# A gated product on one core: loads and stores dealt out by tile to two DMA queues instead of one queue for each direction

## The chip, the core and the metric

The kernel runs on one core of a Trainium2 chip. A core has a tensor engine (PE), a vector engine (VectorE, DVE in the profile), a scalar engine (ScalarE, ACT), a general engine (GpSimd, POOL) and a sync engine (SyncE, SP), each with its own stream of instructions. Data move between the chip's main memory (HBM) and the core's memory of 128 partitions (SBUF) by DMA: an instruction on SP or ACT issues a transfer, which then runs on 16 DMA engines that all of the core's queues share. The profile calls the queue of SP's transfers q1 and that of ACT's q10. Waits go by semaphores, which an instruction or a landed transfer raises.

The metric is the device time of one execution in microseconds (us), less is better. Times are the median of several executions; the profile comes from one further execution of the same program.

## The reference

The input is 8192 x 8192 in 32-bit floats. The left half of the columns is multiplied by the sigmoid of the right half:

```python
def reference(x):
    a, b = np.split(x, 2, axis=-1)
    return a * (1 / (1 + np.exp(-b)))
```

So 268.4 MB are read and 134.2 MB are written, and each element takes one sigmoid and one product.

## The kernel before

The 8192 rows are cut into 32 tiles of 256 rows. Each of the 128 partitions holds two whole rows of a tile, which lie next to each other in HBM: 64 KB a partition, 8 MB a tile. The result of a tile is half as large, 32 KB a partition and 4 MB. There are two input buffers (`x_sb0`, `x_sb1`) and two output buffers (`o_sb0`, `o_sb1`); even tiles use the first of each, odd tiles the second.

For each tile the work is a load, a sigmoid in place over the right halves on ACT (L92), the product in two pieces (L97), and a store. The product of the first 3/16 of the columns is done by POOL (by DVE in tile 1), and that of the rest by DVE, which starts when POOL is done. The first and the last tile are worked on in fourths (half a row each, all products on DVE) so that a store can start earlier. Tile 0 is loaded in two transfers, one for each of the two rows of a partition, and stored in two; tile 31 is stored in three pieces (one half, two quarters), of which each is issued one fourth late.

A helper, `place`, drops all dependences but those that are listed, and keeps the program's order on each engine. Four waits are left:

- load i+2 waits for the last product of tile i, which frees the input buffer (`free`, L62);
- the sigmoid of tile i waits for the landing of load i and, from tile 2 on, of store i-2, which frees the output buffer. Both are joined by an empty instruction on PE (`met`, L87), so that ACT waits for one semaphore;
- the product follows the sigmoid, DVE's piece follows POOL's;
- store i waits for the products of tile i (`done`, L69).

All loads are issued by SP (L63), all stores by ACT (L68), so loads stand in one queue and stores in the other. The order of the instructions is written out by the last loop of `_tiles`: the work of tile i, then load i+2, then what is left to store of tile i. ACT's stream thus has, tile after tile, the sigmoid and then the store, at which ACT stands until the product is done. Loads 0 and 1 are issued ahead of the loop, without waits. After the program is built, `_launch_early` moves the first load on SP to before the start barrier, and `_close_on_sync` writes the end anew: the last store's semaphore is awaited on SP, all the others on POOL.

Of the kernel before, what the change touches and what calls it, by code (L numbers as in the profile page):

```python
# [8 lines left out]
def _tiles(ctx, tc, x, out):  # L9
    nc = tc.nc  # L10
    P = nc.NUM_PARTITIONS
    DEP = mybir.DependencyInfo(mybir.DependencyClass.Sync, mybir.DependencyReason.DATA)
    fp32 = mybir.dt.float32
    SIG = mybir.ActivationFunctionType.Sigmoid

    n_rows, n_cols = x.shape
    half = n_cols // 2
    R = 2
    SLOTS = 2
    n_tiles = n_rows // (P * R)  # L20
    x_g = x.rearrange("(g p h r) m -> g h p (r m)", p=P, h=2, r=R)
    out_g = out.rearrange("(g p h r) m -> g h p (r m)", p=P, h=2, r=R)

    pool = ctx.enter_context(tc.tile_pool(name="io", bufs=1))
    xs = [pool.tile([P, R * n_cols], fp32, name=f"x_sb{k}") for k in range(SLOTS)]
    os = [pool.tile([P, R * half], fp32, name=f"o_sb{k}") for k in range(SLOTS)]

    whole = [(0, 8)]
    rows = [(0, 4), (4, 8)]
    cut = half // 16 * 3  # L30
    few_and_most = [(0, 8, 0, cut), (0, 8, cut, half)]
    fourths = [(k, k + 2, k % 4 * half // 4, (k % 4 + 2) * half // 4) for k in range(0, 8, 2)]
    loads = [whole] * n_tiles
    works = [few_and_most] * n_tiles
    stores = [whole] * n_tiles
    behind = [0] * n_tiles
    loads[0] = stores[0] = rows
    works[0] = works[-1] = fourths
    stores[-1] = [(0, 4), (4, 6), (6, 8)]
    behind[-1] = 1  # L40

    def meet(a, b):
        return a[0] < b[1] and b[0] < a[1]

    traced = [[] for _ in range(SLOTS)]
    load_of, mul_of, store_of = {}, {}, {}

    def place(i, ins, *needs):


        kept = {n.ins.name for n in needs}
        for e in traced[i % SLOTS]:
            if e.ins.name not in kept:
                tc.declare_no_dep(ins.ins, e.ins, reason="follows from the waits that are kept")
        traced[i % SLOTS].append(ins)
        tc.keep_in_program_order(ins)
        return ins

    def load(i):
        for lo, hi in loads[i]:  # L60
            c = slice(lo * n_cols // 4, hi * n_cols // 4)
            free = [m for w, m in mul_of.get(i - SLOTS, []) if meet(w, (lo, hi))]  # L62
            ins = nc.sync.dma_start(out=xs[i % SLOTS][:, c], in_=x_g[i // 2, i % 2, :, c])  # L63
            load_of.setdefault(i, []).append(((lo, hi), place(i, ins, *free)))

    def store(i, lo, hi):
        c = slice(lo * half // 4, hi * half // 4)
        ins = nc.scalar.dma_start(out=out_g[i // 2, i % 2, :, c], in_=os[i % SLOTS][:, c])  # L68
        done = [m for w, m in mul_of[i] if meet(w, (lo, hi))]  # L69
        store_of.setdefault(i, []).append(((lo, hi), place(i, ins, *done)))  # L70

    def work(i, lo, hi, near, far):

        rows = xs[i % SLOTS].rearrange("p (r h m) -> p r h m", r=R, h=2)
        packed = os[i % SLOTS].rearrange("p (r m) -> p r m", r=R)
        r, c = slice(lo // 4, (hi + 3) // 4), slice(near, far)
        b = rows[:, r, 1, c]
        landed = [s for w, s in load_of[i] if meet(w, (lo, hi))]
        gone = [s for w, s in store_of.get(i - SLOTS, []) if meet(w, (lo, hi))]
        middle = 0 < i < n_tiles - 1  # L80
        rest = middle and near
        if rest:
            before = mul_of[i].pop()[1]
        else:
            g = rows[:, r, 1, :] if middle else b
            if middle and gone:
                met = nc.tensor.nop(nofuse=True)  # L87
                for n in (*landed, *gone):
                    tc.add_manual_dep(met.ins, n.ins.name, DEP, reason="joins the waits")
                place(i, met, *landed, *gone)  # L90
                landed = [met]
            before = nc.scalar.activation(out=g, in_=g, func=SIG)  # L92
            for n in landed:
                tc.add_manual_dep(before.ins, n.ins.name, DEP, reason="both have landed")
            place(i, before, *landed)
        engine = nc.gpsimd if far == cut and i > 1 else nc.vector
        mul = engine.tensor_mul(out=packed[:, r, c], in0=rows[:, r, 0, c], in1=b)  # L97
        tc.add_manual_dep(mul.ins, before.ins.name, DEP, reason="follows the gate, or the first columns")
        place(i, mul, before, *(() if middle else gone))
        mul_of.setdefault(i, []).append(((lo, hi), mul))  # L100

    for i in range(SLOTS):
        load(i)
    for i in range(n_tiles):
        due = list(stores[i])
        for k, piece in enumerate(works[i]):
            work(i, *piece)
            ready = works[i][k - behind[i]][1] if k >= behind[i] else 0
            while len(stores[i]) > 1 and k < len(works[i]) - 1 and due[0][1] <= ready:
                store(i, *due.pop(0))  # L110
        if i + SLOTS < n_tiles:
            load(i + SLOTS)
        for lo, hi in due:
            store(i, lo, hi)


def _launch_early(nc):
# [68 lines left out]
@with_exitstack  # L186
def kernel(
    ctx: ExitStack,
    tc: tile.TileContext,
    x: bass.AP,  # L190
    out: bass.AP,
):
    nc = tc.nc
    with ExitStack() as pools:
        _tiles(pools, tc, x, out)
    tc.close()
    tc.compile()
    _launch_early(nc)
    _close_on_sync(nc)
# [30 lines left out]
```

## Time and profile before

| | us |
|---|---|
| median of 3 executions | 932.75 (932.47 to 932.77) |
| the profiled execution, its time | 932.44 |
| its span, from the first instruction to the last | 931.1 |
| DVE busy | 232.5 |
| ACT busy | 227.0 |
| POOL busy | 99.3 |
| the sigmoid of a whole tile on ACT | 7.03 |
| POOL's piece of a product | 3.42 |
| DVE's piece of a product | 7.09 |
| a load, from issue to landing, median | 40.0 |
| a store of 4 MB, from issue to landing, median | 40.2 |

The page of the profile gives busy times for each engine, the share of DMA time in 40 slices of the span as digits (9 is 90% or more), the packets of each DMA queue, the chain of work that ended last, and the transfers by line with the time from issue to landing. A transfer's issue is short (0.3 to 0.4 us); its data move afterwards on the 16 engines, and its packets are recorded there with a start and a duration. The time from issue to landing includes what lies ahead of the transfer in its queue. Lines such as L92 are line numbers of the kernel before. "ACTq" and "SPq" are the streams of ACT and SP where they issue transfers.

### The profile page before, as it was taken

The page shows a single profiled execution, that of the slowest core. Times are in us where ns is not written, and L with a number is a line of the kernel's source. Part 1 is how long each engine was busy: PE and PEld are TensorE (multiplying, and loading weights), DVE is VectorE, ACT ScalarE, POOL GpSimd, SP SyncE. Part 2 cuts the span into 40 slices and gives each one's busy share as a digit, 9 for nine tenths or more (in the row PEclk, how much of TensorE's full clock was granted, in tenths as well). Part 3 has the DMA queues.
Part 4 walks back from the last instruction along what each step waited for, and adds up shares of the span by engine and source line. Part 5 has one row for each costly group of instructions (what it writes and reads, how often), then busy time and mean ns, then how long its engine had stood idle before and what let it go on. Part 6 is the DMA issues. An engine that isn't in the chain of part 4 may idle for free.

```text
span 931.1 us, 299 instructions
## 1 busy us (share of the span) xinstructions
DVE 232.5 (25%) x39; ACT 227.0 (24%) x39; POOL 99.3 (11%) x33
## 2 busy tenths in 40 slices
DVE  1133203332023320233302333023330233311333
ACT  2123332033320333202332023320233202333023
POOL 0001110111101111011110111101111011110110
DMA  9999999999999999999999999999999999999998
GB/s 405 450 442 414 428 450 425 453 405 428 450 428 450 410 469 405 428 450 428 450 405 459 420 428 451 425 450 408 431 448 428 450 408 467 408 428 450 427 452 383
DMA packets 9793, 402.67 MB, mean 432 GB/s; under 512 B 1088, under 2 KB 1088, under 8 KB 1088
## 3 DMA queue, kind: packets, MB, share of 16 engines
q1 hardware_dynamic: 4752, 268.44, 66.6%
q10 hardware_dynamic: 5040, 134.22, 33.4%
q14 instruction: 1, 0.01, 0.0%
HBM read 268.44 MB, written 134.22 MB: 432 GB/s over the span
## 4 chain that ended last, share of the span: by engine, by line
DMA 69%; DVE 12%; ACT 12%; POOL 5%; issue 0%; PEldq 0%; ACTq 0%; SPq 0%
DMA out_dram<-o_sb 60%; DVE o_sb L97 12%; ACT x_sb L92 12%; DMA x_sb<-in_x_dram 9%; POOL o_sb L97 5%; PEldq L87 0%; ACTq L68 0%; SPq L63 0%
## 5 line engine op out<-in xcount | busy, mean ns | idle before, releaser
L97 DVE TENSOR_TENSOR o_sb<-x_sb 128x6656 f32<-128x6656 f32 (+2 forms) x39 | 232.5, 5969 | 690.3 <-POOL o_sb L97 632.7
L92 ACT ACTIVATE x_sb<-x_sb 128x8192 f32<-128x8192 f32 (+1 forms) x38 | 225.7, 5949 | 692.7 <-PEq L87 632.9
L97 POOL TENSOR_TENSOR o_sb<-x_sb 128x1536 f32<-128x1536 f32 x29 | 99.1, 3417 | 793.9 <-ACT x_sb L92 793.9
L92 ACT ACT_TABLE_LOAD x1 | 1.3, 1283 | 0.8 <-PEq L214 0.8
L214 POOL MEMSET const-float32-0.0<- 128x1 f32 x1 | 0.1, 99 | 0.2 <-issue 0.2
L214 POOL MEMSET const-bfloat16-1.0<- 128x1 bf16 x1 | 0.1, 103 | 0.0
L214 POOL MEMSET const-uint8-127<- 128x1 uint8 x1 | 0.1, 103 | 0.0
L214 POOL MEMSET const-float32-1.0<- 128x1 f32 x1 | 0.1, 99 | 0.0
## 6 DMA issues: line engine op xcount, KB each, us to landing
out_dram<-o_sb ACTq DMA_DIRECT2D x30, 4096.0 KB, 40.2
x_sb<-in_x_dram SPq DMA_DIRECT2D x2, 4096.0 KB, 16.6
out_dram<-o_sb ACTq DMA_DIRECT2D x3, 2048.0 KB, 27.8
out_dram<-o_sb ACTq DMA_DIRECT2D x2, 1024.0 KB, 8.3
x_sb<-in_x_dram SPq DMA_DIRECT2D x31, 40.0
```

What stands on the lines that cost most here:

```text
L92: before = nc.scalar.activation(out=g, in_=g, func=SIG)
L97: mul = engine.tensor_mul(out=packed[:, r, c], in0=rows[:, r, 0, c], in1=b)
L214: nc = _bacc.Bacc("TRN2", target_bir_lowering=False, num_devices=1)
```

## The change

The queue of a transfer now goes by its tile: loads and stores of even tiles are issued by SP, those of odd tiles by ACT. Within a tile the order is turned round: the store of tile i is issued first, and then load i+2, in the same queue. Load 1, which had no wait, now waits for the first of the two transfers of load 0. Tile 0 is stored in one transfer when all of it is done. The compute instructions remain, in the same order on each engine. On ACT, the first instruction is now load 1 with its wait, ahead of the load of the sigmoid's table, and the loads of tiles 3, 5, ... 31 each stand right behind the store of the tile two before; 15 stores of whole even tiles leave ACT's stream, and so do the two half stores of tile 0, and all 16 whole even-tile stores stand in SP's.

```diff
+    queues = [nc.sync, nc.scalar]
     whole = [(0, 8)]
     rows = [(0, 4), (4, 8)]
...
-    loads[0] = stores[0] = rows
+    loads[0] = rows
     works[0] = works[-1] = fourths
...
             free = [m for w, m in mul_of.get(i - SLOTS, []) if meet(w, (lo, hi))]
-            ins = nc.sync.dma_start(out=xs[i % SLOTS][:, c], in_=x_g[i // 2, i % 2, :, c])
+            if i == 1:
+                free = [load_of[0][0][1]]
+            ins = queues[i % 2].dma_start(out=xs[i % SLOTS][:, c], in_=x_g[i // 2, i % 2, :, c])
+            if i == 1:
+                tc.add_manual_dep(ins.ins, free[0].ins.name, DEP, reason="one tile behind")
             load_of.setdefault(i, []).append(((lo, hi), place(i, ins, *free)))
 
     def store(i, lo, hi):
         c = slice(lo * half // 4, hi * half // 4)
-        ins = nc.scalar.dma_start(out=out_g[i // 2, i % 2, :, c], in_=os[i % SLOTS][:, c])
+        ins = queues[i % 2].dma_start(out=out_g[i // 2, i % 2, :, c], in_=os[i % SLOTS][:, c])
...
+        for lo, hi in due:
+            store(i, lo, hi)
         if i + SLOTS < n_tiles:
             load(i + SLOTS)
-        for lo, hi in due:
-            store(i, lo, hi)
```

## The prediction

> **What bounds the kernel now.** First I read the page's head and its DMA parts (slices, queues, issues).
>
> ```profile
> span 931.1 us, 299 instructions
> ...
> DVE 232.5 (25%) x39; ACT 227.0 (24%) x39; POOL 99.3 (11%) x33
> ...
> DMA  9999999999999999999999999999999999999998
> DMA packets 9793, 402.67 MB, mean 432 GB/s; under 512 B 1088, under 2 KB 1088, under 8 KB 1088
> ...
> q1 hardware_dynamic: 4752, 268.44, 66.6%
> q10 hardware_dynamic: 5040, 134.22, 33.4%
> ...
> out_dram<-o_sb ACTq DMA_DIRECT2D x30, 4096.0 KB, 40.2
> ...
> out_dram<-o_sb ACTq DMA_DIRECT2D x3, 2048.0 KB, 27.8
> ...
> x_sb<-in_x_dram SPq DMA_DIRECT2D x31, 40.0
> ```
>
> No engine is busy more than a quarter of the span, while the 16 DMA engines are busy in every slice. Loads (q1) and stores (q10) are never both absent. Next, two windows of a whole 29 us tile period, where columns are DVE, ACT, POOL busy, clock, DMA share and GB/s:
>
> ```profile
> 100.00:129.00 29.00, 7.09 (x1) 6.70 (x1) 3.42 (x1) 1.00 1.00 434
> ...
> 500.00:529.00 29.00, 7.09 (x1) 7.03 (x1) 3.42 (x1) 1.00 1.00 434
> ```
>
> The DMA share is 1.00 early and late alike. Then the chain of waits, one tile and the end of the run (start, length, what):
>
> ```profile
> 813.60 40.21 DMA out_dram<-o_sb
> ...
> 853.92 7.04 ACT x_sb L92
> ...
> 861.03 3.43 POOL o_sb L97
> ...
> 864.48 7.10 DVE o_sb L97
> ...
> 871.60 40.04 DMA x_sb<-in_x_dram
> ...
> 911.66 1.92 ACT x_sb L92
> ```
>
> (871.60 is also when store 29 goes out.) From landing (813.60 + 40.21 = 853.81) to the next issue it takes 871.60 - 853.81 = 17.8 us. Last, the timeline around the fill of the pipeline and at the end:
>
> ```profile
> 18.57 0.38 ACTq L68 DMA_DIRECT2D out_dram<-o_sb  x1
> ...
> 28.28 0.36 ACTq L68 DMA_DIRECT2D out_dram<-o_sb  x1
> 46.23 7.03 ACT L92 ACTIVATE x_sb<-x_sb 128x8192 f32<-128x8192 f32 x1 [20.70 <-DMA x_sb<-in_x_dram]
> ...
> 918.13 0.34 ACTq L68 DMA_DIRECT2D out_dram<-o_sb  x1
> ...
> 920.33 2.79 ACTq L68 DMA_DIRECT2D out_dram<-o_sb  x2
> ```
>
> The trace's packet records, which the page only sums up, give the prices. Each DMA puts 8 packets on each engine. A 64 KB packet (whole load) takes 2.418 us, a 32 KB one (whole store, or a row of load 0) 1.213, a 16 KB one 0.611, an 8 KB one 0.309. One engine carries 16 x 1.213 + 248 x 2.418 + 240 x 1.213 + 24 x 0.611 + 16 x 0.309 = 929.8 us; its first packet starts at 0.98 and the last ends at 930.75, which is 929.8 as well. So before has no DMA gap at all, not even at its two ends. The durations are equal with loads alone (2 to 20 us: 1.213), with stores alone (912 to 920 us: 1.213) and mixed. Hence the change can gain only what it takes off the packets, and loses every stretch in which both rings are empty.
>
> The profiled execution took 932.44 us, 1.34 more than its span; the median is 932.75, 0.31 above it. The sum is made on the span and carried over by these two.
>
> **The change part by part.**
>
> *Bytes and queues.* Every load and store remains, in the same sizes, but for store 0: one of 4 MB instead of two of 2 MB, 8 x 1.213 = 9.70 us per engine for 16 x 0.611 = 9.78: -0.07. Sixteen loads move from SP to ACT, sixteen stores from ACT to SP (two of them become the one). An issue takes 0.33 us on SP and 0.36 on ACT. ACT has 692.7 us of idle, SP does nothing else: 0. The order store i, load i+2 makes the load's issue 0.4 us later; both waited for the same multiply before. It lies behind the store's 8 packets in its ring anyway: 0. What is queued behind a waiting store on ACT is the sigmoid of the next even tile, whose data come later than that multiply as long as the rings alternate: 0. The sigmoid no longer waits for a store that lands last (157.58 against 157.40 for the load issued with it), as store i-2 is now ahead of load i in the same ring.
>
> *How two rings share.* Store 0's first row, 8 packets of 16 KB issued at 18.57, landed at 46.39, when load 1 did (46.21): one 16 KB packet for each 64 KB one. Whole stores and loads issued together land together too (40.2, 40.0). So the engines take packets in turn, one from each ring. The Trainium skill, "DMA: Bandwidth & Descriptors", section "Queues, rings and completion order", has a round robin of whole packets, typically 9 to 17 descriptors before a switch. The trace disagrees if a descriptor is one of these records: the switch comes after every one. By the page's figure a DMA's 8 would go through uncut, tile 0's second row would land at 21.8 as before, and neither the fill below nor the rival on it would have a price.
>
> *The steady state.* A ring now has per cycle of two tiles (58.1 us): compute, store (9.7 us of packets), load (19.3). From the last load packet to the next store's first packet it is empty for 0.4 (row 0's last packet ends at 11.7, row 0 lands at 12.08) + 17.8 + entry. Entry, from issue to first packet, has two rows: the launch (0.00 to 0.98..1.53) and store 0's first row (18.57 to 23.56: 5.0 us, three packets having started after the issue). Among 64 KB packets three would be up to 1.2 + 3 x 2.418 = 8.5 us. The other ring covers 8 x (2.418 + 1.213) = 29.06 us. Needed: 0.4 + 17.8 + 1.0..8.5 = 19.2 to 26.7. Slack 2.4 to 9.9: no gap, 0 per tile. I take an entry of 5.6 us, nearer the busy row: 23.8 empty, (29.06 - 23.8) / 3.631 = 1.5 packet pairs of overlap at each hand-over. A switch from store to load within a lone ring isn't shown. Across rings the direction changes at every packet and costs nothing; from load 0's first row to its second, alone, there is no gap: 0. Its upper end is the launch's first packet, which took up to 2.15 instead of 1.21: 0.94 x 30 = 28 us.
>
> *The fill.* Load 1, before third in SP's ring, is now issued on ACT when row 0 has landed (12.08). By the busy row three row-1 packets start after the issue (12.7, 13.9, 15.1; the one of 11.4 is already running), so load 1 enters at 16.3 with four of row 1's packets left. In turn they take 4 x 3.631 = 14.5: row 1 ends at 30.8, not 21.4, and tile 0 stores at 30.8 + 0.4 + 6.5 (21.80 to 28.28) = 37.7. Load 1's last packet ends at 21.3 + 8 x 2.418 = 40.6 in any case. Store 0 can enter at 37.7 + 1.0..2.24 (the latter from 918.13 to 920.37, when the packets of the piece followed without a gap) = 38.7 to 39.9: before 40.6, no gap: 0. With the launch's entry (1.0) load 1 comes at 13.9, six packets are left, row 1 ends at 35.7, store 0 enters at 43.6 to 44.8: a gap of 3.0 to 4.2. That is the upper end; the lower is 0. I take 0, as the busy row is the like case. The activation table's load (1.28 us, before at 0.77 us) now stands behind load 1's wait on ACT. It delays row 0's gates by 1.7 us; row 1's at 31 us cover it, and would not if row 1 landed at 17.
>
> *The end.* Before, store 30 was wholly left at 911.6 and covered the 6.5 us until store 31's first piece. Now store 30 has its own ring and is 1.5 packets ahead when load 31 ends: 6.5 x 1.213 = 7.9 us are left. The first piece enters at 0.4 + 6.5 + 1.0..2.24 = 7.9 to 9.1 after that: a gap of 0 to 1.2, taken as 0.6. With entry 1.0 to 2.3 pairs of overlap, 6.9 us are left and the gap is 2.2 at most.
>
> Sum: -0.07 + 0 + 0 + 0.6 = +0.5 on 931.1 gives a span of 931.6 and 932.75 + 0.5 = 933.3 as the time. The ends: -0.07 to +4.2 + 2.2 = 6.4, 932.7 to 939.1 (the store-to-load switch apart).
>
> **The rivals.**
>
> *The pipeline fills late* (slower). Load 1 cuts in sooner than three packets, row 1 is starved, and tile 0's single store comes after load 1 has ended. For: nothing else is queued then, since store 0 no longer goes out at 18.6. Against: the 5.0 us row. It decides, with 0.6 of the end, when the gap exceeds 1.3 us, that is when load 1 enters by 15.1 or before: five packets left, row 1 ends at 33.3, store 0 enters at 41.2 to 42.4, 0.6 to 1.8. Time 934.7 to 939, middle 936. Chance 0.31.
>
> *The rings fall in step* (much slower). If entry exceeded 29.06 - 18.2 = 10.9 us, both would be empty at once, at worst 19 us for each of 15 pairs: 290 us. Against: the slack above. The Trainium skill, "Perfetto Trace Analysis", section "DMA Optimizations", advises one issuing engine for inputs and another for outputs, which is what the change gives up; its sum, if any, would lie here. No row of before bears out a loss, since the other ring covers a load held behind a store. Chance 0.03.
>
> *The switch from store to load costs* in a lone ring: up to 28 us, 961; a third of that 942. Against: the free change of direction across rings. Chance 0.05.
>
> *Faster.* It would take 1.87 us (0.2%), thus 7.5 ns off each of the 248 load packets. They take the same 2.418 throughout and twice 1.213 but for 8 ns. Time 930.5, chance 0.03.
>
> **How the numbers follow.** 0.2% of 932.75 is 1.87 us, about what a measurement of this kernel can tell from no change. My forecast, 933.3, within 932.4 to 934.6, has 0.58: same. Fill, step and switch make slower 0.39, the last rival faster 0.03. The range runs from 932.3 (no gap, and the 0.3 us by which runs of before differ) to 938.5 (both gaps nearly whole); outside lie step, switch, faster and the far end of the fill: about 0.13.
>
> **What the new profile would show.** DMA share 1.00 in 29 us windows, each queue with about half the bytes. Stores land in 17 to 21 us instead of 40.2, loads still in about 40; the chain runs over loads, not stores. Row 1 of tile 0 is ready at 30 to 32 us, store 0 is issued near 37.7, and no idle DMA around 41. Load 31 lands at 913 to 915 and store 31's first piece follows 6.5 us later. Wrong would be: row 1 after 33 us with a DMA hole near 41 (fill), a share below 0.99 in the middle (switch), or sigmoids further apart than 29 us (step).

## The result and the profile after

The changed kernel takes 940.98 us (median of 4, 940.48 to 941.86) against 932.61 us (932.42 to 932.77): a ratio of 1.0091, with a 95% interval of 1.0078 to 1.0103. It is 8.4 us slower; 933.3 was predicted, and the range ended at 938.5. The profiled execution's span is 940.1 us, 9.0 above the one before.

The page of the changed kernel, its DMA parts and its chain of waits:

```profile
span 940.1 us, 268 instructions
...
DMA  9999999999999999999999999999999999999998
...
DMA packets 9649, 402.67 MB, mean 428 GB/s; under 512 B 1072, under 2 KB 1072, under 8 KB 1072
...
q1 hardware_dynamic: 4752, 201.33, 50.0%
q10 hardware_dynamic: 4896, 201.33, 49.7%
...
DMA x_sb<-in_x_dram 69%; DVE o_sb L102 12%; ACT x_sb L97 12%; POOL o_sb L102 5%; ACTq L73 1%; PEldq L92 0%
...
out_dram<-o_sb SPq DMA_DIRECT2D x16, 4096.0 KB, 17.3
out_dram<-o_sb ACTq DMA_DIRECT2D x15, 4096.0 KB, 18.7
...
x_sb<-in_x_dram ACTq DMA_DIRECT2D x16, 40.3
x_sb<-in_x_dram SPq DMA_DIRECT2D x15, 40.1
```

The shape is the one foretold: both queues move half the bytes, stores land in 17 to 19 us instead of 40, the chain runs over loads, and the DMA engines still look busy in every slice. The loss is too thin for the digits. The timeline shows where the fill and the end went:

```profile
11.99 0.38 ACTq L66 DMA_DIRECT2D x_sb<-in_x_dram  x1
...
33.78 3.71 ACT L97 ACTIVATE x_sb<-x_sb 128x2048 f32<-128x2048 f32 x2 [16.38 <-DMA x_sb<-in_x_dram]
...
40.25 0.35 SPq L73 DMA_DIRECT2D out_dram<-o_sb  x1
...
912.25 0.34 SPq L73 DMA_DIRECT2D out_dram<-o_sb  x1
922.31 5.51 ACT L97 ACTIVATE x_sb<-x_sb 128x2048 f32<-128x2048 f32 x3 [20.70 <-DMA x_sb<-in_x_dram]
...
928.77 0.34 ACTq L73 DMA_DIRECT2D out_dram<-o_sb  x1
```

Row 1 of tile 0 is ready at 33.8 us (21.8 before), store 0 goes out at 40.25, load 31 lands at 922.3 (911.6 before). Windows of the same execution (DVE, ACT, POOL busy, clock, DMA share, GB/s):

```profile
39.00:42.00 3.00, 1.22 (x1) 0.96 (x1) 0.00 (x0) 1.00 0.41 175
...
500.00:529.00 29.00, 8.22 (x2) 7.03 (x1) 3.42 (x1) 1.00 1.00 432
...
925.00:929.50 4.50, 4.50 (x3) 3.16 (x3) 0.00 (x0) 1.00 0.27 117
```

The kernel before, around the landing of load 1 and at the first store of tile 31:

```profile
22.00:46.00 24.00, 4.49 (x2) 3.53 (x2) 0.00 (x0) 1.00 1.01 437
...
918.00:921.00 3.00, 2.84 (x3) 1.91 (x1) 0.00 (x0) 1.00 0.98 421
```

A window counts a packet where it starts, so short ones are rough; but there is a hole around 41 us and one ahead of 929.5 us, which before does not have. In the middle the share is 1.00 as before, at 432 GB/s instead of 434. A share of 1.00 doesn't exclude a loss: a packet that takes longer is busy for longer.

To place the loss I took from the packet records, at a moment of the run, the time that has passed less the packets done so far (mean over the 16 engines, each packet at the price of the kernel before: 2.418, 1.213, 0.611, 0.309 us). What that lag grows by in a stage is DMA time lost there, be it idle or in packets that take longer. The numbers are us; the start of the run counts to the fill, and the end goes to the last packet:

```
                 fill, to 65 us   middle, 65 to 915   end, from 915   sum
before                1.86             -1.25              0.34         0.95
changed               4.31              2.16              3.51         9.98
changed - before     +2.45             +3.41             +3.17        +9.03
```

(The middle of before is below zero because its records overlap by a few ns a packet.) The sum is the 9.0 us of the two spans. So there are three losses of about the same size, where I had foretold 0, 0 and 0.6. They differ in kind: from 65 to 915 us the engines of the changed kernel are idle for 0.02 us, as before, and all of the middle's loss is in longer packets (64 KB packets together 3.2 us too long on the mean engine, 32 KB packets 0.3); idle time is 0.7 us at 41 us and 3.3 us ahead of store 31.

The fill, in packets of the changed kernel (queue, bytes, number of engines, first and last start; the 4-byte records are the completion marks that make up a landing):

```
q1  32768 x16 start 14.84 to 15.25
q10 65536 x12 start 16.05 to 16.45     load 1 comes in
...
q1  32768 x12 start 29.33 to 29.74     row 1's last packet on 12 engines
q10 65536 x16 start 30.54 to 30.95
q1  4     x12 start 32.95 to 33.37     row 1's completion marks there
...
q10 65536 x16 start 37.79 to 38.21     load 1's last packet
q1  32768 x16 start 41.10 to 41.24     store 0 comes in
...
q1  65536 x16 start 58.89 to 59.22     load 2, took 3.27 to 3.54
```

Load 1 came in at 16.05 (foretold 16.3) and row 1's data ended at 30.95 (30.8). But the completion mark is a record of its own and waited its turn behind another 64 KB packet of load 1: 2.4 us. From 33.76 on all was as worked out: store 0 issued 6.5 us later, in the engines 0.85 us after that, and a hole of about 0.7 us. Then store 0's packets took 0.8 us longer than 8 x 1.213 in all, nearly all of it (0.75) on the last packet, ahead of load 2 in a ring that ran alone: it took 1.69 to 2.32 us instead of 1.213. And load 2's packet that was running when store 1 came in took about 1 us longer on every engine.

The end, in the same form, for load 31's completion marks and the packets around them:

```
before    q1  4     x16 start 910.67 to 911.29     load 31
          q10 32768 x16 start 919.15 to 919.77     store 30's last packet
          q10 16384 x16 start 920.37 to 920.97     store 31's first piece
changed   q10 4     x10 start 915.22 to 915.51     load 31 on ten engines
          ...
          q10 4     x4  start 921.53 to 921.86     load 31 on the last four
          q1  4     x10 start 924.90 to 925.19     store 30 done on ten engines
          ...
          q1  4     x4  start 928.80 to 929.13     store 30 done on the last four
          q10 16384 x16 start 929.61 to 929.76     store 31's first piece
```

A load has landed when the slowest engine is done. Before, load 31 is completed within 0.6 us by all engines; now within 6.65. Two things add up to that. When store 30 ends nothing else is left and every engine has moved the same bytes, so its marks show how far apart the engines are in their work: 924.90 to 929.13, 4.2 us. The other 2.4 us are two of store 30's packets (2 x 1.213), which the late engines took in turn ahead of load 31's completion mark, the second one between the last data packet and the mark. Ten engines are done with everything at 925 and stand idle for 4.5 us, until the product that waited for the last four. The last four wait for 0.5 to 0.8 us.

### The profile page after: what moved, and what is told of

The parts are those of the page before. It is cut to its first block, busy times and chain, and to the rows that moved or that the text cites. A ratio compares the mean times of both kernels' runs of the same rounds, so it can differ in the third digit from the quotient of the medians.

```text
span 940.1 us, 268 instructions
## 1 busy us (share of the span) xinstructions
DVE 232.5 (25%) x39; ACT 227.0 (24%) x39; POOL 99.3 (11%) x33
## 4 chain that ended last, share of the span: by engine, by line
DMA 69%; DVE 12%; ACT 12%; POOL 5%; ACTq 1%; issue 0%; PEldq 0%
DMA x_sb<-in_x_dram 69%; DVE o_sb L102 12%; ACT x_sb L97 12%; POOL o_sb L102 5%; ACTq L73 1%; PEldq L92 0%
```

## The experiments

The first four take the losses apart. The table has all the twelve runs, with the lag's growth by stage, how far apart the 16 engines complete load 31 ("load") and store 30 ("engines"), for the runs that bear on these; the median of before was 932.57 to 932.71 beside them. Where "load" is clearly larger than "engines", it is so by one or two packets of 1.213 us.

Time and ratio are medians; the other columns come from the one execution that was profiled. The kernels by tile scatter more than the one before (940.48 to 941.86 for the changed one), and two profiled executions lay 1.2 us or more above all others of their kernel: 942.47 with store 30 on ACT, 939.05 with the switch at tile 6. The fill repeats well (4.24 to 4.31 in the four runs that leave it as changed), but 1 us or so between two rows in the middle or at the end may be scatter.

```
                                    time  ratio (95% interval)      fill  middle   end  load  engines
before                            932.61                            1.86   -1.25  0.34   0.6      0.6
changed                           940.98  1.0091 (1.0078-1.0103)    4.31    2.16  3.51   6.7      4.2
load 1 on SP, no wait             939.37  1.0071 (1.0057-1.0084)    3.10    2.02  3.44   6.9      4.5
store 30 on ACT                   940.25  1.0088 (1.0074-1.0102)    4.29    3.27  3.47   4.5      4.4
both                              938.96  1.0070 (1.0057-1.0082)    3.37    1.32  2.82   4.2      4.2
load first in the tile's queue   1179.36  1.2646 (1.2629-1.2663)
before, store first               932.62  1.0000 (0.9991-1.0009)
load 1 without its wait           952.26  1.0208 (1.0194-1.0222)   11.00    6.75  2.86   4.6      3.4
back to direction at tile 6       937.56  1.0055 (1.0042-1.0068)    4.24    0.04  3.32   4.9      3.6
all on one queue                  938.66  1.0060 (1.0046-1.0074)    3.06    0.96  3.88   6.1      6.2
half tiles, by direction          937.36  1.0050 (1.0034-1.0067)
half tiles, by tile               937.95  1.0056 (1.0041-1.0071)
back to direction at tile 3       935.86  1.0036 (1.0023-1.0048)    4.29   -0.98  1.29   2.2      0.9
before, by tile from tile 24      939.15  1.0068 (1.0055-1.0082)    2.07    1.55  3.97   5.4      3.0
```

**The fill undone.** Load 1 goes back to SP, right behind load 0.

```diff
-            if i == 1:
-                free = [load_of[0][0][1]]
-            ins = queues[i % 2].dma_start(out=xs[i % SLOTS][:, c], in_=x_g[i // 2, i % 2, :, c])
-            if i == 1:
-                tc.add_manual_dep(ins.ins, free[0].ins.name, DEP, reason="one tile behind")
+            ins = queues[i % 2 if i > 1 else 0].dma_start(out=xs[i % SLOTS][:, c], in_=x_g[i // 2, i % 2, :, c])
```

> Load 1 is put back on SP without its wait; everything else is the changed kernel. Theory (three separate losses: about 1.6 us in the fill, 4.5 us in packets that are stretched when a transfer enters a ring that has run empty, 3.3 us of idle DMA in the tail): row 1 of tile 0 lands at 22 us instead of 33.8, store 0 is queued before load 1 ends, no idle DMA at 40 us, and the time falls by about 1.6 us to 939.4. Rival (the loss belongs to the steady state, and a gap in the fill only shifts the phases of the two rings): no gap at 40 us, but the time stays at 941.

939.37: the time fell by the 1.6 us named, but only partly for the reason named. Store 0 was issued at 28.17 us and queued behind load 1 in the same ring, so there was no idle time at 40 us. But load 1's last packet took 3.43 to 3.95 us instead of 2.418. The store had been waiting for 12 us, so this is no late start: it is a price for going from a run of loads to a store. The step after it, from store 0's last packet to load 2 in the same ring, cost nothing here.

**The end changed.** Store 30 alone moves to ACT, behind load 31.

```diff
-        ins = queues[i % 2].dma_start(out=out_g[i // 2, i % 2, :, c], in_=os[i % SLOTS][:, c])
+        ins = queues[i % 2 if i < n_tiles - 2 else 1].dma_start(out=out_g[i // 2, i % 2, :, c], in_=os[i % SLOTS][:, c])
```

> Store 30 alone is put on ACT, behind load 31 in its ring; everything else is the changed kernel. Theory: store 30 no longer shares with load 31, is left whole when load 31 ends, and covers the 6.5 us until store 31's first piece, so the idle stretch of the tail (3.3 us) goes: 937.7. Rival (the engines are already apart before the tail, so load 31 lands late on the slowest ones whatever store 30 does): idle of over 2 us stays and the time is 940 or more.

940.25, and 3.47 us lost at the end as before the edit: the rival holds. Thirteen engines completed load 31 by 917.8, one at 918.6 and two at 921.2 to 921.3, though store 30 could no longer take turns with it. The engines were apart already, by 4.4 us; what the edit took off the landing are the two packets in turn. The idle time moved: 1.5 us ahead of store 31 on most engines, and as much at the very end, where they wait for the last two.

This execution also had, from 508 to 860 us, six steps from a load to a store at which the store's first packet took up to 2.2 us instead of 1.213, worth 0.16 to 0.71 us each; that makes its middle 3.27.

**Both edits.**

> Both edits together: load 1 on SP without its wait, and store 30 on ACT. Theory: the two savings add up, 941.0 - 1.6 - 3.3 = 936.1, and what is left over the kernel before (3.5 us) is stretched packets in the steady state with the DMA share at 1.00. Rival: less than 2 us is saved in all, 939 or more.

938.96: 2.0 us saved in all, at the rival's end. The savings do not add up to 4.9, since the second one is hardly any.

**The order undone.** Load i+2 ahead of store i, in the queue of the tile.

```diff
-        for lo, hi in due:
-            store(i, lo, hi)
         if i + SLOTS < n_tiles:
             load(i + SLOTS)
+        for lo, hi in due:
+            store(i, lo, hi)
```

> The order within a tile is undone: load i+2 is issued ahead of store i, in the same queue by tile. Theory (any transfer that enters an emptied ring stretches the packet that runs on the other): the stretched packets of the steady state stay, 3 to 4 us, the tail keeps a gap, and the time is 940 to 942. Rival (it is the store's entry among loads that stretches them): the stretch falls below 1 us and the time to about 938.

Neither theory: 1179.36 us. The windows of this run show the two rings in step:

```profile
101.00:111.50 10.50, 7.09 (x1) 7.03 (x1) 5.47 (x2) 1.00 0.00 0
111.50:172.00 60.50, 7.09 (x1) 3.97 (x1) 2.75 (x1) 1.00 1.00 416
172.00:186.00 14.00, 7.09 (x1) 9.98 (x2) 7.38 (x2) 1.00 0.00 0
```

For 60 us both rings transfer, then for 14 us nothing moves and both tiles are computed at once: 186 - 111.5 = 74.5 us for two tiles instead of 58. The packets in turn fit it. With the store first, the tile that enters has 32 KB packets and the one that ends has 64 KB ones, which get two thirds of the rate, end sooner and so stay ahead. With the load first it is the other way round: the tile that ends is held up by the one that enters, until both end together (stores at 167.91 and 172.91 us, 242.54 and 247.70). The store-first order is what the queues by tile live on. The rival that I called "the rings fall in step", with a chance of 0.03, is real; it is set off by the order, not by a long entry.

**The order alone**, in the kernel before, with its queues by direction (the same edit as in the change, without the rest).

> The kernel before with the order within a tile alone changed: store i is issued (on ACT) ahead of load i+2 (on SP). Theory: the two stand in different queues and wait for the same product, so nothing moves: 932.6, within 0.3 us. Rival: the order as such costs part of the 8.4 us: 934 or more.

932.62 beside 932.71: no effect, as foretold. With separate queues the order is free.

**Load 1 without its wait**, on ACT at once.

```diff
-            if i == 1:
-                free = [load_of[0][0][1]]
...
-            if i == 1:
-                tc.add_manual_dep(ins.ins, free[0].ins.name, DEP, reason="one tile behind")
```

> The changed kernel without load 1's wait for tile 0's first row: load 1 is issued on ACT at once. Theory (packets in turn, fill worked out from rows): both rows of tile 0 lie in turn with load 1's 64 KB packets, row 0 lands at about 31 us, row 1 at 41, store 0 is issued at about 47.5 instead of 40.25, and the idle DMA after load 1 grows from 0.7 to about 7.7 us: 941.0 + 7 = 948, the steady state and the tail as in the changed kernel. Rival (the rings fall in step when both begin together): period per two tiles over 60 us and a time above 1000.

952.26, no falling in step. Row 1 was ready at 41.05 and store 0 issued at 47.51, as worked out (row 0 came at 26.5, not 31); the fill lost 6.7 us more than the changed kernel's, where 7 were named. Not foretold was the middle, which lost 6.75 instead of 2.16. So the wait for the first row is worth 11 us in this arrangement.

**Back to queues by direction from tile 6 on.**

```diff
-            ins = queues[i % 2].dma_start(out=xs[i % SLOTS][:, c], in_=x_g[i // 2, i % 2, :, c])
+            ins = queues[i % 2 if i < 6 else 0].dma_start(out=xs[i % SLOTS][:, c], in_=x_g[i // 2, i % 2, :, c])
...
-        ins = queues[i % 2].dma_start(out=out_g[i // 2, i % 2, :, c], in_=os[i % SLOTS][:, c])
+        ins = queues[i % 2 if i < 6 else 1].dma_start(out=out_g[i // 2, i % 2, :, c], in_=os[i % SLOTS][:, c])
```

> Queues by tile up to tile 5, then by direction as in the kernel before (loads on SP, stores on ACT), the order store first kept. Theory (the 16 engines take their turns differently at each hand-over between the rings, drift apart, and the fast ones stand idle in the tail; the stretched packets also come from hand-overs): after tile 6 there are no hand-overs, the landings of a load stay within 1 us of each other on all engines instead of 6.7, the tail has no gap, and the fill's loss of about 3 us is all that is left: 935.7. Rival (drift and gap come from the fill or from the order): the landings drift as before and the time is 938 or more.

937.56, between the two. Load 6 already landed 4.1 us apart on the engines, and the loads stayed 4.9 apart to the end (4.84 to 4.93 at every load from 311 us on): nothing brings the engines together again as long as none runs out of work. From 200 us on there were hardly any stretched packets (0.2 us in all), and the lag fell as it does before (5.2 at 220 us, 4.28 at 915). The end lost 3.32 all the same.

**All transfers on one queue**, but for tile 31's stores (load 1 without a wait, store first).

```diff
+            ins = nc.sync.dma_start(out=xs[i % SLOTS][:, c], in_=x_g[i // 2, i % 2, :, c])
...
+        ins = queues[i == n_tiles - 1].dma_start(out=out_g[i // 2, i % 2, :, c], in_=os[i % SLOTS][:, c])
```

> All transfers but tile 31's stores go over SP's queue alone, store i ahead of load i+2, so each engine works through pure runs of 8 loads and 8 stores. Theory (the last load packet ahead of a store in a lone ring is stretched by 1.0 to 1.5 us, as at 38 us of the run with load 1 back on SP): 31 changes of direction at about 1.2 us make 932.6 + 37 = 970, all of it in packets of over 3.4 us. Rival (only a transfer that enters an emptied ring is stretched, not a change of direction): 933 to 937, plus whatever idle time there is since store i comes 19.2 us after load i's last packet and load i+1 takes 19.3.

938.66, far from 970. The page of this run has one queue with everything in it:

```profile
out_dram<-o_sb SPq DMA_DIRECT2D x31, 4096.0 KB, 21.0
...
x_sb<-in_x_dram SPq DMA_DIRECT2D x31, 40.2
```

The first change from loads to a store stretched load 1's last packet to 3.31 to 4.10 us, as in the first experiment. The second, at 68 us, reached 2.66 at most. Summed over the engines the load packets were too long by 0.93 us from 66 to 200 us, 0.95 to 400, 0.39 to 600 and 0.02 after that, while the engines went from 0.7 us apart (first load) to 2.9 (at 248 us) and 5.7 (454 us), and stayed at 6.1 from 600 us on. So a change of direction has no fixed price. And the drift needs no second ring: here the engines have nobody to take turns with.

**Half tiles.** One row a partition, four buffers; the same queues as before, and by tile. With it the pieces of the first and the last tile are halves of the smaller tile, and tile 0 is loaded and stored whole. By tile, load 1's wait is left out too.

```diff
-    R = 2
-    SLOTS = 2
+    R = 1
+    SLOTS = 4
...
-    loads[0] = stores[0] = rows
     works[0] = works[-1] = fourths
-    stores[-1] = [(0, 4), (4, 6), (6, 8)]
+    stores[-1] = [(0, 2), (2, 4)]
```

> The kernel before with tiles of half the size (one row a partition) and four buffers instead of two; loads on SP, stores on ACT. It is the reference for the next run. The same bytes keep the DMA engines busy throughout: 932 to 935.

> The same half tiles and four buffers with the changed kernel's queues: by tile, store i ahead of load i+4. Each ring now holds two tiles' transfers and should never run empty. Theory (the loss comes from rings that run empty and from the hand-overs between them): no drift of the engines, no stretched packets, the same time as the half tiles by direction, within 2 us. Rival (queues that mix loads and stores are slower as such): 5 us or more slower than by direction.

937.36 by direction, 937.95 by tile: 0.6 us between them. Both are slower than the 932 to 935 that I wrote for the first, mainly because two small packets take a little longer than a large one: 512 x 1.213 + 504 x 0.611 + 16 x 0.309 = 934.0 us of packets for each engine, 4.2 more than the 929.8 of the kernel before. Queues that mix loads and stores cost next to nothing when each holds two tiles and never runs empty; the lag falls through the middle in both (by tile from 2.55 at 65 us to 0.19 at 915, by direction from 2.30 to -0.34), so there is neither a hole nor a stretch to speak of (packets over 60 ns too long add up to 0.1 us). Only the drift was not wholly gone: the last loads land 2.4 us apart on the engines, against 1.4 by direction. The Trainium skill, "DMA: Bandwidth & Descriptors", section "Issuing engines are not separate DMA queues", says that transfers of all issuers share the engines and interleave, so that the issuer saves issue time only; these two runs agree with it, to 0.6 us.

**Back to direction from tile 3 on**, before the engines are apart (the edit of tile 6 with 3).

> As the run that goes back to queues by direction at tile 6, but already at tile 3 (in the changed kernel the spread of a landing over the engines is 0.5 us there and 4 us at tile 6). Theory (hand-overs make the engines drift apart, and the drift makes the tail's gap): a spread below 1.5 us to the end, less than 1 us of idle DMA in the tail instead of 3.2, the fill's 2.6 us left: 935.3 to 936. Rival (the gap in the tail has another cause than the drift): 2 us or more of idle in the tail and 937 or more.

935.86, as the theory had it. The loads land 2.1 to 2.2 us apart (a little more than the 1.5 named; the engines themselves are 0.9 apart at store 30), the middle loses 0.27 us against before, and the end 0.95 us more than before instead of 3.17.

**By tile only from tile 24 on**, in the kernel before with the store first.

```diff
-            ins = nc.sync.dma_start(out=xs[i % SLOTS][:, c], in_=x_g[i // 2, i % 2, :, c])
+            ins = queues[i % 2 if i >= 24 else 0].dma_start(out=xs[i % SLOTS][:, c], in_=x_g[i // 2, i % 2, :, c])
...
-        ins = nc.scalar.dma_start(out=out_g[i // 2, i % 2, :, c], in_=os[i % SLOTS][:, c])
+        ins = queues[i % 2 if i >= 24 else 1].dma_start(out=out_g[i // 2, i % 2, :, c], in_=os[i % SLOTS][:, c])
```

> The kernel before (store first, loads on SP and stores on ACT) up to tile 23, queues by tile from tile 24 to the end. Theory (16 engines that are close together meet at the change from loads to stores and stretch the last load packets; the stretch fades as they drift apart, not with time): the first changes after 700 us stretch packets by 0.3 to 1 us each as at 59 us of the changed kernel, the spread grows to 2 us or more within the last tiles, and the time is 935 to 938. Rival (the stretch belongs to the beginning of the run): 0.1 us or less per change, as the changed kernel has at that time, no drift, 933 to 934.

939.15, more than either named. With the engines 0.6 us apart the first two changes of direction cost 0.50 us (716 to 718 us) and 1.08 (725 to 733) in longer packets; the changed kernel has about 0.1 each at that time. The first of the two is a step from a store to a load in ACT's queue, with 0.34 us of it on the store's last packet. The ones after those cost 0.08, 0.10, 0.02, 0.34, 0.35 and 0.30. The first load after them landed 2.2 us apart on the engines and load 31 5.4 apart (the engines themselves 1.0 and 3.0), and the end lost 3.97. So the stretch does not belong to the beginning of the run, and eight tiles suffice for 6.5 of the 8.4 us.

## Why the prediction was wrong

*Right, by its steps.* Nothing could be gained: the DMA engines had no gap before, and no run was faster. The packets keep their prices whether loads, stores or both run (2.418 and 1.213 are the medians of both queues). Records go in turn, one from each ring, and load 1 entered the fill at 16.05 us for 16.3. The entry into a ring with the other one busy took 4.6 to 5.7 us for 5.6 (store 14, issued at 445.71, started at 450.27 to 451.42), and 2.7 to 6.5 over all stores from tile 1 to tile 30, inside the 1.0 to 8.5 reckoned with. The two rings always covered each other: no idle time in the middle. With queues by direction the order cost nothing. The moved issues delayed nothing, though 18 load issues were recorded at 3.1 to 5.5 us where the prediction had 0.33 and 0.36: their engines had nothing else to do meanwhile.

*The fill* was put at 0 with an upper end of 4.2; it was 2.45. The step that failed is the landing: 0.4 us after the last packet, taken from a row where the ring had no competitor. With load 1 in turn, row 1's completion mark waited one more 64 KB packet (2.4 us). By the prediction's own entry (1.0 to 2.24 us) store 0 had a margin of 0.7 to 1.9 us ahead of load 1's end, so this delay is enough for the hole of 0.7. The rest are store 0's last packet (0.75), which is the switch below, and the stretched packet at 58.9 us (1.0). The loss lies inside the stated bounds of the fill, but not by their mechanism, an early entry of load 1. The sign named for the fill did come: row 1 after 33 us and a hole near 41.

*The switch* was put at 0 with an upper end of 28 us and a chance of 0.05. It was 3.41 us over the middle, and 1.7 of the fill's loss. The step that failed is that I priced one direction only, from store to load. That one did cost: 0.75 us at 49.6 us (up to 1.11 on an engine, where the upper end had 0.94), and part of 0.50 in the run by tile from tile 24; but in the middle of the changed kernel and in the one-queue run it cost nothing. What costs again and again is the step from a run of loads to a store, mostly on the last load packet, and it had no term at all. The sign that I named for it, a DMA share below 0.99, could not show it, because a stretched packet counts as busy. The trace of before held a hint: when store 0's first row came in beside loads alone, at 20.8 to 21.3 us, load 1's first packets took up to 2.78 us instead of 2.42. I read that store for its entry and not for what it did to its neighbour.

*The end* was put at 0.6 with an upper end of 1.2 to 2.2; it was 3.17. The step that failed is that 16 engines were treated as one. My rows gave store 30's rest and store 31's entry, but a landing is the slowest engine's, and 6.65 us between them was in no row of before (at most 0.7 there). For the slowest engines the step holds: the gap there is 0.5 to 0.8 us, for 0.6. The other engines are done with store 30 earlier, which makes 2.8 us on the mean of all 16; with the gap of the slowest that is the idle time of 3.3 us ahead of store 31. The pair of runs that go back to direction, with the same end, agrees: engines 3.6 us apart lose 3.32, 0.9 apart 1.29. (The first of these was the slowest execution of its kernel; by their medians the two runs are 1.7 us apart.)

*The rivals.* "The pipeline fills late" happened to a third of the loss, and not by an early entry of load 1. "The rings fall in step" did not happen, yet one edit of the order brings it about. The Trainium skill's advice in "Perfetto Trace Analysis", section "DMA Optimizations", to give inputs and outputs an issuing engine each, points the right way here: by direction whole runs had 0.2 to 0.7 us of longer packets after the first 12 us, the changed kernel 5.3, and their last loads landed 0.6 to 1.4 us apart on the engines. I had counted it under a rival of 0.03, because I looked for idle rings only.

What stays open: what in the engines stretches a packet at a change of direction, and why it does so unequally from engine to engine, which is where the drift would come from. The stretch is large (about 1 us) when the engines are less than 1 us apart, at 40 us as well as at 720, and falls to nothing in the one-queue run once they are 5.7 apart. That they disturb each other by changing direction together would fit, but no run took the drift away while keeping the changes, so it is argued, not shown. One row speaks against a simple fading: with store 30 on ACT, a step at 624 us cost 0.71 us when the engines were about 5 us apart, though 14 of the 16 ended that load within 0.5 us of each other. No version beat the kernel before, whose engines have no gap up to the last packet.

## What to carry to other kernels

When the DMA engines are saturated, ask of a new queue layout three things beyond idle time: whose record does a completion mark wait behind, how often does an engine go from a run of loads to a store, and how far apart are the engines when the last landing releases the last work. In this kernel one ring for loads and one for stores, each with the next transfer always queued, answers all three. If queues must mix, the runs here speak for keeping two transfers' worth in each (half tiles), and, where each holds one tile, for issuing the store ahead of the load.

## What the runs showed of the hardware

The 16 engines of one core drift apart while all are busy, in the changed kernel by up to 4.7 us (completion marks of its stores, with the other ring empty) and in the one-queue run by 6.2, and stay apart until they run out of work; before, they were at most 0.73 apart. Packets taken in turn come on top: loads of the changed kernel landed 6.6 to 7.2 us apart on the engines from 690 us on. A completion mark takes its own turn: behind a busy ring with 64 KB packets a landing came 2.8 us after the last data packet (30.95 to 33.76), with no other ring 0.4. And the order in which a tile's store and the next load are issued, worth 0.1 us or less with queues by direction (932.62 against 932.71), is worth 238 us (1179.36 against 940.98) with queues by tile.
